# A product of the coming units behind each transpose of attention, in a fixed order

## The chip, the cores and the metric

The kernel runs on one core of a Trainium2 chip. The metric is the time of one launch in microseconds of the device; the times shown are the median of three runs. The engines that matter here are TensorE (PE: matmuls, with the weight loads shown as PEld), VectorE (DVE), ScalarE (ACT), GpSimd (POOL) and the queue of SyncE (SP), which issues most loads.

## The reference

One hybrid decoder block on x of 512 x 1024, float32: an RMS norm, one wide input projection, two attention branches of 8 heads of 64 each, and a gated merge with an output projection and a residual add.

```python
h = rms_norm(x, norm_g)
fq, fk, fv, fz, mq, mk, mv, mz, ga, gb, fl = split_cols(h @ w_in, IN_SPLITS)
q, k = rms_norm(heads(fq), fox_q_g), rms_norm(heads(fk), fox_k_g)
log_f = log_sigmoid(fl + b_f)                     # causal decay, cumulated over positions
y_fox = softmax(q k^T * scale + c_i - c_j, causal) v * silu(fz)
q, k = rope(rms_norm(heads(mq), moba_q_g)), rope(rms_norm(heads(mk), moba_k_g))
y_moba = softmax over the own block of 256 (causal) and up to 3 chosen earlier blocks * silu(mz)
merged = sigmoid(ga + b_gate0) * (y_fox @ w_fox) + sigmoid(gb + b_gate1) * (y_moba @ w_moba)
out = x + merged @ w_out
```

With 512 positions there are two blocks of 256, so the chosen blocks are all the earlier ones and the moba branch is a plain causal softmax too.

## The kernel before

Every float32 product is made of three matmuls in the fp32r type: an operand is split into a high part (a copy by ACT: the names wh, Gh, QS, KH, pth) and a low part (a subtraction, mostly by DVE: wl, Gl, KL, ptl), and high x high, high x low and low x high are accumulated in one PSUM tile.

**Units.** The input projection is cut into units. A unit of fq, fk, fv, mq, mk or mv (`unit`) makes one block of 128 positions and 256 columns: 8 k-tiles x 3 = 24 matmuls of 256 columns into a PSUM tile with tag `pj`, of which there are two, and then its copy out (`evac_qk`, `evac_v`). A unit of fz or mz (`unit_z`) makes 24 matmuls of 512 columns, one of w_fox (`unit_f`) 12 of 512 columns. I call their matmuls products. `unit_mm` (L308), `tr_mm` (L407) and `br_mm` (L691) issue them; L315 to L317, L414 to L416 and L696 to L698 are their lines in the profile. A chunk of weights is loaded by SP and split ahead of use by `pump` (L189), which is called before each unit.

**Attention.** There are four groups of four heads (fox a, fox b, moba a, moba b), each of two pairs. `Tr(pr)` (L526) transposes q and k of a pair: four transposes into the PSUM tile p_qT (L530) and four into p_kT (L532); ACT and DVE then make QS, KH, KL of each head from these two tiles. `Aa(h)` makes the logits of a head, four PSUM tiles lg (tag `lg`, two buffers) of 128, 256, 384 and 512 columns, two matmuls each (L572, L573); DVE takes the maximum and ACT the exp, into p0 to p3. `Bb(h)` (L610) transposes the ten blocks of p that the causal mask leaves (L617, by `blk`): four into p_a, four into p_b, two into p_cc; each tile is split by `spl` into pth (ACT) and ptl (DVE), and pv is accumulated from them in a fixed order (L627, L628). p_qT, p_kT, p_a, p_b, p_cc and p_ri (the transpose of the inverse sums) share the tag `tp` of three PSUM buffers; pv has one buffer.

**What sets the order.** Each engine runs its own queue in order. A scheduler lays the instructions of the program on the engines, by readiness in its own estimate and by their place in the program; `tc.issue_after(i)` ties an instruction behind instruction i on its engine, and `behind()` (L119) ties behind the last one that the program issued on an engine. In the program the pieces of attention (`Tr`, `Aa`, `Bb`, `Yp`) alternate with units (`inter`, L1034): while group n is computed, the units that group n + 1 needs are the filler (`plan`, L1074). The scheduler is free to put the units' products between the transposes, logits and pv matmuls as these become ready.

Of the kernel before, what the change touches and what calls it, by code (L numbers as in the profile page):

```python
# [13 lines left out]
P = 128  # L14
# [15 lines left out]
def fox_moba_kernel(ctx: ExitStack, tc, xT, x, w_in, w_fl, w_fox, w_moba, w_out, cst, rope, out):  # L30
# [60 lines left out]
    def col(c, n=1):  # L91
        return cs[:, c:c + n]
# [212 lines left out]
        for i, (a, b) in enumerate(pairs):  # L305
            T.matmul(o, a, b, start=(i == 0), stop=(i == n - 1))

    def unit_mm(p, name, t, hfs=(0, 1), first=True, last=True):  # L308
        n = 264 if name == "fka" else CW
        for hf in hfs:  # L310
            hi, lo = chunks[name][hf]
            for k in range(4):
                kk = 4 * hf + k
                st = slice(t * P, (t + 1) * P)
                T.matmul(p[:, :n], Gh[:, kk, st], hi[:, k, :n], start=(kk == 0), stop=False)  # L315
                T.matmul(p[:, :n], Gh[:, kk, st], lo[:, k, :n], start=False, stop=False)
                T.matmul(p[:, :n], Gl[:, kk, st], hi[:, k, :n], start=False, stop=(kk == KT - 1))  # L317

    def evac_qk(p, name, t):
        if name not in QN:  # L320
# [75 lines left out]
    def unit(name, t):  # L396
        def go():
            p = pj(f"pj_{name}{t}")
            unit_mm(p, name, t)
            if name[1] == "v":  # L400
                evac_v(p, name, t)
            else:
                evac_qk(p, name, t)
        return go


    def tr_mm(p, name, c):  # L407
        cc = slice(c * P, (c + 1) * P)
        for hf in range(2):
            hi, lo = chunks[name][hf]  # L410
            for k in range(4):
                kk = 4 * hf + k
                gh, gl = Z[kk] if name[0] == "f" else (Gh[:, kk, :], Gl[:, kk, :])
                T.matmul(p, hi[:, k, cc], gh, start=(kk == 0), stop=False)  # L414
                T.matmul(p, hi[:, k, cc], gl, start=False, stop=False)
                T.matmul(p, lo[:, k, cc], gh, start=False, stop=(kk == KT - 1))  # L416

    ZS = {}

# [2 lines left out]
    def unit_z(name, c):  # L422
        def go():
            p = (tp if name == "fzb" else pj)(f"pz_{name}{c}")
            tr_mm(p, name, c)
            z = t2("y", 15, f"zs_{name}{c}")
            s = t2("y", 15, "sg") if name == "mzb" else t2("u", 4, "sg")
            if name[0] == "f":
                V.tensor_tensor(out=z, in0=p, in1=rbc, op=OP.mult)
                A.activation(s, z, AF.Tanh, scale=0.5)  # L430
                V.scalar_tensor_tensor(z, s, 1.0, z, op0=OP.add, op1=OP.mult)
            else:
                A.activation(s, p, AF.Tanh, scale=0.5)
                V.scalar_tensor_tensor(z, s, 1.0, p, op0=OP.add, op1=OP.mult)
            ZS[name[0], 2 * (name[2] == "b") + c] = z
        return go


    LR = con.tile([64, S], F32R, name="LR")
# [77 lines left out]
    def attn_group(br, half, gq, gk):  # L517
# [8 lines left out]
        def Tr(pr):  # L526
            def go():
                pq, pk = tp("p_qT"), tp("p_kT")
                for t in range(NT):
                    T.transpose(pq[:, t * P:(t + 1) * P], qn[:, t, pr * P:(pr + 1) * P], ident)  # L530
                for t in range(NT):
                    T.transpose(pk[:, t * P:(t + 1) * P], kn[:, t, pr * P:(pr + 1) * P], ident)  # L532
                for o in range(2):
                    h = 2 * pr + o
                    me, ot = (slice(0, HD), slice(HD, P)) if o == 0 else (slice(HD, P), slice(0, HD))
                    qs = t2("qs", 4, "QS", dt=F32R)
                    kh = t2("qs", 4, "KH", dt=F32R)
                    kl = KLt[o][pr]
                    A.activation(qs[me, :], pq[me, :], AF.Copy, scale=gq[me, :])
                    V.scalar_tensor_tensor(qs[ot, :], pq[me, :], gq[me, :], qs[me, :].bitcast(F32),  # L540
                                           op0=OP.mult, op1=OP.subtract)
                    A.activation(kh[me, :], pk[me, :], AF.Copy, scale=gk[me, :])
                    if direct:
                        A.activation(kh[ot, :], pk[me, :], AF.Copy, scale=gk[me, :])  # L544
                    else:
                        nc.scalar.dma_start(out=kh[ot, :].bitcast(F32), in_=kh[me, :].bitcast(F32))
                    V.scalar_tensor_tensor(kl[me, :], pk[me, :], gk[me, :], kh[me, :].bitcast(F32),  # L547
                                           op0=OP.mult, op1=OP.subtract)
                    q2 = qs
                    if fox:  # L550
                        q2 = Q2t[o]
                        lr = slice(HD, HD + 4) if o == 0 else slice(0, 4)
                        hh = hb + h
                        nc.sync.dma_start(out=q2[lr, :].bitcast(F32), in_=LR[hh:32:8, :].bitcast(F32))
                        nc.sync.dma_start(out=kl[lr, :].bitcast(F32), in_=LR[32 + hh:64:8, :].bitcast(F32))
                        if direct:
                            V.tensor_copy(q2[me, :], qs[me, :].bitcast(F32))
                        else:
                            nc.scalar.dma_start(out=q2[me, :].bitcast(F32), in_=qs[me, :].bitcast(F32))
                    st[h] = (qs, kh, kl, q2)  # L560
            return go
# [48 lines left out]
        def Bb(h):  # L610
            def go():
# [2 lines left out]
                pv = pst("pv", 1, "pv")  # L614

                def blk(dst, i, j):
                    T.transpose(dst, pts[i][:, j * P:(j + 1) * P], ident)  # L617

                def spl(p, n):
                    tag, w, bufs = ("pt", 512, 4) if n == 512 else ("pc", 256, 2)  # L620
# [67 lines left out]

    FS, MG = {}, {}

    def br_mm(p, name, br, c):  # L691
        hi, lo = chunks[name][0]
        cc = slice(c * P, (c + 1) * P)
        for k in range(4):
            yh, yl = Y[br, k]
            T.matmul(p, hi[:, k, cc], yh, start=(k == 0), stop=False)  # L696
            T.matmul(p, hi[:, k, cc], yl, start=False, stop=False)  # L697
            T.matmul(p, lo[:, k, cc], yh, start=False, stop=(k == 3))  # L698

    def unit_f(i, c):  # L700
        def go():
            j = 2 * i + c
            p = pj(f"pf{j}")
            br_mm(p, f"wf{i}", "f", c)
            if j == 0:
                f = sb.tile([P, 4, S], F32, name="f03", tag="v", bufs=2)
                FS[0], FS[1] = f[:, 0:2, :], f[:, 2:4, :]
            elif j in (4, 6):
                FS[j // 2] = sb.tile([P, 2, S], F32, name=f"f{j}", tag="qk", bufs=4)
            A.activation(FS[i][:, c, :], p, AF.Copy)  # L710
        return go
# [121 lines left out]
    def merge_a(i, c):  # L833
        if True:
            j = 2 * i + c
            p = pj(f"pm{j}")
            br_mm(p, f"wm{i}", "m", c)
            u = SG[i][:, c, :]
            V.tensor_tensor(out=u, in0=p, in1=u, op=OP.mult)
            V.tensor_tensor(out=u, in0=u, in1=FS[i][:, c, :], op=OP.add)  # L840
# [180 lines left out]
            return [unit_z(name, c) for c in range(2)]  # L1021
        return [unit(name, t) for t in range(4)]

    def filler(names):
        res = []
        for nm in names:
            for n, u in enumerate(units(nm)):
                def go(i=first_prep[nm] + (n if nm[0] == "G" else 0), u=u):
                    pump(i)
                    u()  # L1030
                res.append(go)
        return res

    def inter(a, b):  # L1034
# [30 lines left out]
    for k, u in enumerate(fz):  # L1065
        u()
        if k < 3:
# [7 lines left out]
            ("f", "b", C_FQ, C_FK, ["mka", "mva", "mza"]),  # L1075
            ("m", "a", C_MQ, C_MK, ["mqb", "mkb", "mvb"]),
            ("m", "b", C_MQ, C_MK, ["mzb", "wf0", "wf1", "wf2"]))
    head, body, tail, gate = attn_group("f", "a", col(C_FQ), col(C_FK))
    head[0]()
    for n in range(4):  # L1080
        nxt = []

        def following(n=n, nxt=nxt):
            br, half, cq, ck = plan[n + 1][:4]
            if n == 1:
                moba_begin()
            nxt.extend(attn_group(br, half, col(cq), col(ck)))
            nxt[0][0]()
        fill = filler(plan[n][4])
        if n == 0:  # L1090
            for k in range(4):
                store = []

                at = 3 * k

                def with_sums(u=fill[at], k=k, store=store):
                    u()
                    with tc.issue_after(last_on(mybir.EngineType.DVE)):
                        store.append(make_sums(k))

                def with_store(u=fill[at + 1], store=store):
                    u()
                    store[0]()
                fill[at], fill[at + 1] = with_sums, with_store
        inter(body + ([following] if n < 3 else []) + tail, fill)
        if n < 3:
            at = 2
            body, tail = nxt[1][:at] + gate + nxt[1][at:], nxt[2]
            gate = nxt[3]
    seq(["wf3"])  # L1110
    enter("gates")
    load_sums()
    fill = filler(["GA0", "GA1", "GB0"])
# [123 lines left out]
```

## Time and profile before

| what | value |
|---|---|
| median of three runs | 425.62 us (425.09 to 425.78) |
| the profiled execution | 425.94 us, span 424.2 us |
| granted TensorE clock | 0.999 |
| PE busy | 417.8 us |
| DVE busy | 327.4 us |
| ACT busy | 279.2 us |
| matmuls | 2913 |

The span runs from the first to the last instruction; about 1.7 us of the execution lie outside it. A row of the groups reads: line, engine, operation, out<-in, shapes, count, then busy time, mean of one in ns, and the idle time just before them with what ended it. A row in order of time reads: start, length, engine, line, operation, tiles, shapes, count. The length of a matmul includes its passage through the array, in which the next one already runs; the distance between two starts is what one costs. Attention lies between 66 and 285 us.

### The profile page before, as it was taken

The numbers are of one execution on the slowest core, as the hardware profiler recorded it, in microseconds if no ns is written. First come the engines' busy times: TensorE is split into PE (matmuls) and PEld (weight loads), VectorE is DVE, ScalarE is ACT, GpSimd is POOL, SyncE is SP. The second block draws the span as 40 slices with busy tenths as digits, with TensorE's granted clock in tenths as the row PEclk, the third lists the DMA queues.
The fourth block names the chain that finished last, engine by engine and source line by source line (L and its number), as shares of the span: only waits on it lengthen the run. The fifth ranks groups of instructions, "written<-read, shape, count | busy, mean of one in ns | idle before, by whom it ended". The sixth has DMA issues, their size and how long they took to land.

```text
span 424.2 us, 7682 instructions
## 1 busy us (share of the span) xinstructions
PE 417.8 (98%) x2913; PEld 388.6 (92%) x2913; DVE 327.4 (77%) x574; ACT 279.2 (66%) x527; POOL 103.8 (24%) x120
## 2 busy tenths in 40 slices
PE   8999999999999999999999999999999999999996
PEld 6998899999999998899998888899999989988885
DVE  3779977799967778678666679767979698689883
ACT  4976326778777878569757687656756535686450
POOL 1065630225235550015660100340000000022230
PEclk9999999999999999999999999999999999999999
DMA  7972334667253033212032310673052703697484
GB/s 233 392 281 87 112 100 111 181 206 199 74 176 114 26 102 100 80 45 99 27 100 68 106 53 27 229 250 117 24 178 62 236 2 110 208 259 118 99 140 159
DMA packets 24340, 56.10 MB, mean 132 GB/s; under 512 B 2808, under 2 KB 7600, under 8 KB 24304
## 3 DMA queue, kind: packets, MB, share of 16 engines
q1 hardware_dynamic: 13392, 38.11, 27.9%
q0 software_dynamic: 3392, 8.39, 8.7%
q10 hardware_dynamic: 7520, 9.11, 6.7%
q8 instruction: 23, 0.38, 0.4%
q14 instruction: 13, 0.11, 0.1%
HBM read 48.11 MB, written 6.32 MB: 128 GB/s over the span
## 4 chain that ended last, share of the span: by engine, by line
PE 96%; DMA 1%; SPq 0%; DVE 0%; issue 0%; ACT 0%
PE pb_GB L770 3%; PE pb_GA L770 3%; PE pb_GA L767 3%; PE pb_GB L767 3%; PE pb_GB L769 3%; PE pb_GA L769 3%; PE po L958 3%; PE po L957 3%; PE po L956 3%; PE pv L628 2%; PE lg L573 2%; PE pv L627 2%; PE lg L572 2%; PE pf L697 2%; PE pf L696 2%; PE pm L698 2%
## 5 line engine op out<-in xcount | busy, mean ns | idle before, releaser
L343 POOL TENSOR_TENSOR ff<-ss,mh 128x8 f32<-128x8 f32 x16 | 31.6, 1981 | 71.4 <-DVE ss L341 62.9
L575 DVE CUSTOM_DVE_ANT_0 p<-lg,mask 128x128 f32<-128x128 f32 (+1 forms) x64 | 30.9, 487 | 16.1 <-PE lg L573 15.6
L577 ACT ACTIVATE p<-p,negm 128x128 f32<-128x128 f32 (+1 forms) x64 | 35.7, 559 | 10.9 <-DVE negm L575 10.0
L905 POOL DMA_DIRECT2D wr_o<-in_w_out_dram x4 | 4.9, 1294 | 95.5 <-ACT wr_o L904 95.5
L143 DVE TENSOR_TENSOR wl_GA<-wr_ga,wh_GA 128x1024 fp32r<-128x1024 f32 x14 | 16.9, 1223 | 5.8 <-ACT wh_GA L141 3.9
L141 ACT ACTIVATE wh_GA<-wr_ga 128x1024 fp32r<-128x1024 f32 x14 | 14.7, 1061 | 9.9 <-PE pb_GA L769 5.1
L141 ACT ACTIVATE wh_GB<-wr_gb 128x1024 fp32r<-128x1024 f32 x14 | 14.6, 1059 | 9.5 <-PE pm L697 3.5
L918 ACT ACTIVATE wh_o<-wr_o 128x1024 fp32r<-128x1024 f32 x14 | 14.8, 1060 | 7.9 <-PE pb_GB L769 2.8
L572 PE MATMUL lg<-KH,QS 128*128 128x128 f32 (+1 forms) x64 | 20.0, 324 | 0.0
L919 DVE TENSOR_TENSOR wl_o<-wr_o,wh_o 128x1024 fp32r<-128x1024 f32 x14 | 17.0, 1222 | 3.8 <-ACT wh_o L918 3.8
L143 DVE TENSOR_TENSOR wl_GB<-wr_gb,wh_GB 128x1024 fp32r<-128x1024 f32 x14 | 16.9, 1222 | 3.5 <-ACT wh_GB L141 3.5
L653 DVE TENSOR_TENSOR ypair<-pv,ysh 64x512 f32<-64x512 f32 x16 | 11.0, 687 | 6.7 <-ACT ysh L652 6.3
L547 DVE SCALAR_TENSOR_TENSOR KL<-p_kT,cs,KH 64x512 fp32r<-64x512 f32 x16 | 12.0, 749 | 3.4 <-ACT KH L544 3.2
L652 ACT ACTIVATE ysh<-pv 64x512 f32<-64x512 f32 x16 | 9.5, 594 | 7.3 <-PE pv L628 4.2
L624 DVE TENSOR_TENSOR ptl<-p_a,pth 128x512 fp32r<-128x512 f32 x16 | 11.0, 685 | 4.2 <-ACT pth L623 4.2
L337 DVE TENSOR_REDUCE ss<-sq 128x8 f32<-128x512 f32 x16 | 10.9, 681 | 4.0 <-ACT sq L336 3.9
L767 PE MATMUL pb_GA<-Gh,wh_GA 128*128 128x256 f32 x48 | 13.6, 284 | 0.0
L769 PE MATMUL pb_GA<-Gl,wh_GA 128*128 128x256 f32 x48 | 13.5, 281 | 0.0
L770 PE MATMUL pb_GA<-Gh,wl_GA 128*128 128x256 f32 x48 | 13.5, 281 | 0.0
L770 PE MATMUL pb_GB<-Gh,wl_GB 128*128 128x256 f32 x48 | 13.5, 281 | 0.0
L769 PE MATMUL pb_GB<-Gl,wh_GB 128*128 128x256 f32 x48 | 13.4, 281 | 0.0
L767 PE MATMUL pb_GB<-Gh,wh_GB 128*128 128x256 f32 x48 | 13.3, 281 | 0.0
(461 smaller groups left out, 1801.8 us busy)
## 6 DMA issues: line engine op xcount, KB each, us to landing
wr_ga<-in_w_in_dram SPq DMA_DIRECT2D x8, 512.0 KB, 3.8
wr_gb<-in_w_in_dram SPq DMA_DIRECT2D x8, 512.0 KB, 4.6
wr_o<-in_w_out_dram SPq DMA_DIRECT2D x8, 512.0 KB, 11.4
xt<-in_xT_dram SPq DMA_DIRECT2D x8, 256.0 KB, 7.3
x<-in_x_dram SPq DMA_DIRECT2D x8, 256.0 KB, 6.0
s_dramh<-sum_sh ACTq DMA_DIRECT2D x8, 256.0 KB, 5.6
s_draml<-sum_sl ACTq DMA_DIRECT2D x8, 256.0 KB, 2.5
wr_wf<-in_w_fox_dram SPq DMA_DIRECT2D x4, 512.0 KB, 3.2
```

What stands on the lines that cost most here:

```text
L141: A.activation(hi[:, :, 0:n], src, AF.Copy)
L143: eng.tensor_tensor(out=lo[:, q, 0:n], in0=src[:, q], in1=hi[:, q, 0:n].bitcast(F32), op=OP.subtract)
L343: G.tensor_tensor(out=f2, in0=ss.rearrange("p t h -> p (t h)"), in1=mh, op=OP.pow)
L572: T.matmul(lg[:, :n], qs[:, qt], kh[:, :n], start=True, stop=False)
L575: V.tensor_tensor_reduce(pt, lg[:, :n], mask[:, 512 - n:512], -0.125, 3.0e38, op0=OP.add, op1=OP.min, accum_out=mkn[:, hh, i:i + 1])
L577: A.activation(pt, pt, AF.Exp, bias=mkn[:, hh, i:i + 1], scale=-1.0, accum_out=rs[:, hh, i:i + 1])
L767: T.matmul(o, hi[:, k, cc], lh, start=(n < 3 and c == 0 and k == 0), stop=False, skip_group_check=True)
L769: T.matmul(o, hi[:, k, cc], ll, start=False, stop=False, skip_group_check=True)
L770: T.matmul(o, lo[:, k, cc], lh, start=False, stop=(k == 3), skip_group_check=True)
L918: A.activation(wide(hi), wide(R[key, c]), AF.Copy)
L919: V.tensor_tensor(out=wide(lo), in0=wide(R[key, c]), in1=wide(hi).bitcast(F32), op=OP.subtract)
L956: T.matmul(o, gh, hi[:, c, r, :], start=(new and k == 0), stop=False, skip_group_check=True)
```

## The change

The functions that issue a unit's products become generators that yield operand pairs, and `products` issues one matmul at each step. A unit becomes an object `Unit` that can be advanced by one product (`step`) or run to its end (`run`). The units that are the filler of attention, and w_fox's last, stand in a list AHEAD in the order of their use. The transposes of q and k and of p go through `turn`: it issues the transpose, tied behind the last instruction issued on PE unless it is the first of its row, and then steps the first unit of AHEAD that is not done, its product tied behind the transpose. What is left of a unit is issued where the unit stood before. The number of transposes and of products is the same, and so are their operands.

```diff
-    def unit_mm(p, name, t, hfs=(0, 1), first=True, last=True):
+    def unit_mm(name, t):
         n = 264 if name == "fka" else CW
-        for hf in hfs:
-            hi, lo = chunks[name][hf]
-            for k in range(4):
-                kk = 4 * hf + k
-                st = slice(t * P, (t + 1) * P)
-                T.matmul(p[:, :n], Gh[:, kk, st], hi[:, k, :n], start=(kk == 0), stop=False)
-                T.matmul(p[:, :n], Gh[:, kk, st], lo[:, k, :n], start=False, stop=False)
-                T.matmul(p[:, :n], Gl[:, kk, st], hi[:, k, :n], start=False, stop=(kk == KT - 1))
+        st = slice(t * P, (t + 1) * P)
+        for kk in range(KT):
+            hi, lo = (w[:, kk % 4, :n] for w in chunks[name][kk // 4])
+            gh, gl = Gh[:, kk, st], Gl[:, kk, st]
+            yield from ((gh, hi), (gh, lo), (gl, hi))
+
+    def products(o, pairs):
+
+        pairs = list(pairs)
+        for i, (a, b) in enumerate(pairs):
+            if i:
+                yield
+            T.matmul(o, a, b, start=(i == 0), stop=(i == len(pairs) - 1))
...
             p = pj(f"pj_{name}{t}")
-            unit_mm(p, name, t)
+            yield from products(p[:, :264 if name == "fka" else CW], unit_mm(name, t))
...
+    AHEAD = []
+
+    def turn(o, i, first):
+        if first:
+            T.transpose(o, i, ident)
+        else:
+            with behind(mybir.EngineType.PE):
+                T.transpose(o, i, ident)
+        while AHEAD and AHEAD[0].done:
+            AHEAD.pop(0)
+        if AHEAD:
+            with behind(mybir.EngineType.PE):
+                AHEAD[0].step()
+
+    class Unit:
+        def __init__(self, i, go):
+            self.i, self.go, self.it, self.done = i, go, None, False
+
+        def step(self):
+            if self.it is None:
+                self.it = self.go()
+            if self.it is None or next(self.it, self) is self:
+                self.done = True
+
+        def run(self):
+            pump(self.i)
+            while not self.done:
+                self.step()
...
                 for t in range(NT):
-                    T.transpose(pq[:, t * P:(t + 1) * P], qn[:, t, pr * P:(pr + 1) * P], ident)
+                    turn(pq[:, t * P:(t + 1) * P], qn[:, t, pr * P:(pr + 1) * P], t == 0)
                 for t in range(NT):
-                    T.transpose(pk[:, t * P:(t + 1) * P], kn[:, t, pr * P:(pr + 1) * P], ident)
+                    turn(pk[:, t * P:(t + 1) * P], kn[:, t, pr * P:(pr + 1) * P], False)
...
                 def blk(dst, i, j):
-                    T.transpose(dst, pts[i][:, j * P:(j + 1) * P], ident)
+                    turn(dst, pts[i][:, j * P:(j + 1) * P], j == 0 and i == 0)
...
-    def filler(names):
+    def filler(names, ahead=False):
         res = []
         for nm in names:
             for n, u in enumerate(units(nm)):
-                def go(i=first_prep[nm] + (n if nm[0] == "G" else 0), u=u):
-                    pump(i)
-                    u()
-                res.append(go)
+                x = Unit(first_prep[nm] + (n if nm[0] == "G" else 0), u)
+                if ahead:
+                    AHEAD.append(x)
+                res.append(x.run)
         return res
...
+    fills = [filler(p[4], True) for p in plan]
+    wf3 = filler(["wf3"], True)
...
-        fill = filler(plan[n][4])
+        fill = fills[n]
...
-    seq(["wf3"])
+    for u in wf3:
+        u()
```

More of the change, by code (lines that the diff above doesn't have):

```diff
@@ L404, in unit, with tr_mm @@
         return go
-    def tr_mm(p, name, c):
+    def tr_mm(name, c):
         cc = slice(c * P, (c + 1) * P)
[L409 to L416, printed above, removed]
+        for kk in range(KT):
+            hi, lo = (w[:, kk % 4, cc] for w in chunks[name][kk // 4])
+            gh, gl = Z[kk] if name[0] == "f" else (Gh[:, kk, :], Gl[:, kk, :])
+            yield from ((hi, gh), (hi, gl), (lo, gh))
     ZS = {}
@@ L424, in go @@
             p = (tp if name == "fzb" else pj)(f"pz_{name}{c}")
-            tr_mm(p, name, c)
+            yield from products(p, tr_mm(name, c))
             z = t2("y", 15, f"zs_{name}{c}")
@@ L689, in fox_moba_kernel, with br_mm @@
     FS, MG = {}, {}
-    def br_mm(p, name, br, c):
+    def br_mm(name, br, c):
         hi, lo = chunks[name][0]
@@ L695, in br_mm @@
             yh, yl = Y[br, k]
-            T.matmul(p, hi[:, k, cc], yh, start=(k == 0), stop=False)
-            T.matmul(p, hi[:, k, cc], yl, start=False, stop=False)
-            T.matmul(p, lo[:, k, cc], yh, start=False, stop=(k == 3))
+            yield from ((hi[:, k, cc], yh), (hi[:, k, cc], yl), (lo[:, k, cc], yh))
     def unit_f(i, c):
@@ L703, in go @@
             p = pj(f"pf{j}")
-            br_mm(p, f"wf{i}", "f", c)
+            yield from products(p, br_mm(f"wf{i}", "f", c))
             if j == 0:
@@ L836, in merge_a @@
             p = pj(f"pm{j}")
-            br_mm(p, f"wm{i}", "m", c)
+            for _ in products(p, br_mm(f"wm{i}", "m", c)):
+                pass
             u = SG[i][:, c, :]
```

## The prediction, on record before the run

> **What bounds the kernel now.** I read the page first, then the list of waits of PE (TensorE's matrix multiply queue), then busy time by stretch, then single instructions in order of time.
>
> ```profile
> span 424.2 us, 7682 instructions
> ...
> PE 417.8 (98%) x2913; PEld 388.6 (92%) x2913; DVE 327.4 (77%) x574; ACT 279.2 (66%) x527; POOL 103.8 (24%) x120
> ...
> PEclk9999999999999999999999999999999999999999
> ...
> PE 96%; DMA 1%; SPq 0%; DVE 0%; issue 0%; ACT 0%
> ```
> ```profile
> PE warm_ps L107 <- DVE fg_pre L480: 1.5, 1, 1.5
> PE fqa L392 <- DVE wl_fqa L168: 0.7, 1, 0.7
> PE fqa L391 <- ACT Zh L131: 0.6, 1, 0.6
> ```
> ```profile
> 66.00:112.00 46.00, 46.00 (x378) 45.31 (x377) 40.98 (x92) 35.12 (x80) 13.00 (x9) 1.00 0.59 169
> 112.00:162.00 50.00, 50.00 (x409) 49.22 (x408) 37.81 (x81) 39.52 (x83) 21.68 (x29) 1.00 0.30 96
> 162.00:216.00 54.00, 54.00 (x394) 50.68 (x393) 40.00 (x83) 40.89 (x88) 17.83 (x21) 1.00 0.27 88
> 216.00:285.00 69.00, 69.00 (x425) 61.16 (x423) 49.44 (x97) 49.00 (x102) 14.48 (x18) 1.00 0.33 108
> ```
>
> The chain that ends last is PE for 96% of the span. The three waits shown are all that PE has, and all lie in the first 12 us. Attention runs from 66 to 285 us, and there PE is busy for the whole of every stretch (46.00 of 46.00, and so on; the columns after the length are PE, weight loads, DVE, ACT, POOL, then clock and DMA). So in attention the time is the sum of what PE is given, and it can change in two ways only: an instruction takes PE less or more time, or PE has to wait. The second has nothing to gain there. VectorE (DVE) and ScalarE (ACT) are not idle: 40.98 and 35.12 of the first 46 us, 37.81 and 39.52 of the next 50.
>
> **Part 1: a product behind each transpose, as a price on PE.** Matmuls overlap, so I price one by the distance between starts.
>
> ```profile
> 66.03 0.60 PE L530 MATMUL p_qT<-ident,qn_fqa 128*128 128x128 f32 x4
> 66.47 0.60 PE L532 MATMUL p_kT<-ident,qn_fka 128*128 128x128 f32 x4
> ...
> 67.03 0.28 PE L316 MATMUL pj_fqb<-wl_fqb,Gh 128*128 128x256 f32 x1
> ...
> 72.47 0.29 PE L317 MATMUL pj_fqb<-wh_fqb,Gl 128*128 128x256 f32 x1
> ...
> 74.92 0.22 PE L572 MATMUL lg<-KH,QS 128*128 128x128 f32 x1
> 74.98 0.28 PE L573 MATMUL lg<-KL,Q 128*128 128x128 f32 x1
> 75.09 0.33 PE L572 MATMUL lg<-KH,QS 128*128 128x256 f32 x1
> ...
> 84.22 0.34 PE L573 MATMUL lg<-KL,Q 128*128 128x384 f32 x1
> 84.39 0.27 PE L617 MATMUL p_a<-ident,p 128*128 128x128 f32 x1
> ...
> 84.62 0.28 PE L316 MATMUL pj_fkb<-wl_fkb,Gh 128*128 128x256 f32 x1
> ```
>
> From 67.03 to 72.47 stand 46 products: 5.44 / 46 = 0.118 us each. From 66.03 to 67.03 stand eight transposes in a row and one product: (1.00 - 0.118) / 8 = 0.110 us a transpose. From 84.39 to 84.62 stand one transpose, alone among other work, and one product: 0.23 - 0.118 = 0.11 us. A transpose alone costs what one in a row does. The change makes rows into single ones, 224 of them (4 groups, each 16 of q and k and 40 of p), 221 of which then have a product next; the count of matmuls and products stays. Price of part 1: 224 x 0 = 0. The bounds: if the next weight load were hidden wholly, a transpose would cost its stream alone, 0.06 us (74.92 to 74.98, also 128 columns): -224 x 0.05 = -11.2 us; if the switch between kinds cost a hundredth of a microsecond, +2.2. I take 0, since the single row at 84.39 is the very case.
>
> [...]
>
> **Part 2: the tied order.** Before, products not yet needed are free work, which the scheduler puts wherever PE would otherwise wait. Now ten of them go with each head's p transposes and eight with each pair's q and k; each such product is held behind its transpose and each transpose but a row's first behind the product ahead of it, and as products of one tile accumulate in order, the rest of that unit is held as well. The program of the changed kernel can be listed by engine, and there free work has gone from several places between a transpose and what needs its copy. A PE instruction that waits for a copy holds the whole queue behind it. I follow four such places, with these prices.
>
> ```profile
> 140.13 0.39 PE L573 MATMUL lg<-KL,Q 128*128 128x512 f32 x1
> 140.36 0.60 PE L532 MATMUL p_kT<-ident,qn_fkb 128*128 128x128 f32 x4
> ...
> 140.99 0.69 ACT L542 ACTIVATE KH<-p_kT,cs 64x512 fp32r<-64x512 f32 x1 [0.22 <-PE p_kT L532]
> ```
> ```profile
> L577 ACT ACTIVATION_READ_ACCUMULATOR p<-p,negm 128x1 f32 x64 | 12.1, 190 | 0.0
> L577 ACT ACTIVATE p<-p,negm 128x512 f32<-128x512 f32 x16 | 11.5, 720 | 1.8 <-DVE negm L575 1.7
> ...
> L542 ACT ACTIVATE KH<-p_kT,cs 64x512 fp32r<-64x512 f32 x16 | 10.9, 680 | 1.2 <-PE p_kT L532 1.0
> ...
> L623 ACT ACTIVATE pth<-p_a 128x512 fp32r<-128x512 f32 x16 | 9.5, 595 | 0.6 <-PE p_a L617 0.3
> ...
> L141 ACT ACTIVATE wh_mza<-wr_mza 128x1024 fp32r<-128x1024 f32 x2 | 2.1, 1060 | 0.0
> ...
> L680 ACT ACTIVATE yhm<-ypair 128x512 fp32r<-128x512 f32 x3 | 1.9, 629 | 2.0 <-DVE ypair L679 2.0
> L599 ACT ACTIVATE rinv_t<-p_ri 8x128 f32<-8x128 f32 x7 | 1.8, 260 | 3.2 <-PE p_ri L597 2.5 <-PE lg L573 0.7
> ...
> L322 ACT ACTIVATE qn_fkb<-pj_fkb 128x256 f32<-128x256 f32 x4 | 1.5, 379 | 0.0
> ```
> ```profile
> L540 DVE SCALAR_TENSOR_TENSOR QS<-p_qT,cs,QS 64x512 fp32r<-64x512 f32 x16 | 12.0, 750 | 1.5 <-ACT QS L539 1.0
> ...
> L624 DVE TENSOR_TENSOR ptl<-p_a,pth 128x512 fp32r<-128x512 f32 x16 | 11.0, 685 | 4.2 <-ACT pth L623 4.2
> ...
> L575 DVE CUSTOM_DVE_ANT_0 p<-lg,mask 128x256 f32<-128x256 f32 x16 | 6.7, 420 | 4.0 <-PE lg L573 4.0
> ...
> L575 DVE CUSTOM_DVE_ANT_0 p<-lg,mask 128x128 f32<-128x128 f32 x16 | 4.6, 288 | 3.5 <-PE lg L573 3.3
> ...
> L143 DVE TENSOR_TENSOR wl_mza<-wr_mza,wh_mza 128x1024 fp32r<-128x1024 f32 x2 | 2.5, 1226 | 0.8 <-ACT wh_mza L141 0.7
> ...
> L557 DVE CAST Q<-QS 64x512 fp32r<-64x512 f32 x4 | 2.1, 536 | 0.1
> ```
>
> The last of four transposes starts at 140.36 + 3 x 0.11 = 140.69 and ACT takes up its tile at 140.99: a lag of 0.30. QS on ACT and KL on DVE have KH's and QS's shapes, so I give them 0.68 and 0.75. A matmul of 512 columns stands 0.23 apart (140.13 to 140.36), one of 384 0.17, one of 128 0.11.
>
> *Place C, the fox b group's second pair.* Time 0 is the start of the last p_kT transpose. PE then has 17 products, four pairs of p_a transpose and product, four lg matmuls: p_b's first transpose is due at 0.11 + 2.01 + 0.91 + 0.45 = 3.48. Its tile comes free when DVE has read p_qT for the second head. ACT, in its order: 0.30, KH 0.98, KH 1.66, wh_mza 2.72, QS 3.40, qn_mka 3.78, wh_mza 4.84, KH 5.52, KH 6.20, pth 6.80. DVE: wl_mza 2.72 to 3.95, QS 4.70, Q 5.23, the p of lg 128 with 0.08 for its sums 5.60, wl_mza 6.83, the p of lg 256 7.33, KL 8.08. So p_b waits 4.70 - 3.48 = 1.22; four pairs and lg 384 twice bring PE to 5.95, and pv waits for pth until 6.80: 0.85; lg 512 then stands at 7.03 and waits for the second p, 7.33: 0.30; after its 0.46, p_cc stands at 7.79 and waits for KL, 8.08: 0.29. Sum 2.7 us. Before, 23 products stand between p_a and p_b here, 23 x 0.118 = 2.7 us of cover.
>
> *Place B, the moba b group's first pair.* From the last p_qT transpose to pv listed 1.6 us (two pairs of p_kT, four of p_a, the products); ACT in that order does QS 0.68, yhm 0.63, an exp 0.72 + 0.19, pth 0.60 after the lag of 0.30: 3.1. Wait 1.5. Then p_b needs p_a's tile, which ptl frees 0.69 after pth; 0.68 later its last transpose starts, lag and pth 0.90: 2.27, where the list has 0.23 + 0.91 + 0.23 = 1.37. Wait 0.9.
>
> *Place E, the moba b group's second pair.* From the last p_kT transpose to p_b listed 0.34 + 4 x 0.34 + 0.45 = 2.15; p_qT comes free after lag, KH, KH, QS on ACT and QS on DVE: 0.30 + 3 x 0.68 + 0.75 = 3.09. Wait 0.9.
>
> *Place A, fox a.* Of fkb the second unit's end has moved behind the third's. ACT copies it out after rinv_t: from p_ri's start 0.30 + 0.26 + 0.38 = 0.94, and the product that takes that tile is listed 0.11 after p_ri. Wait 0.8.
>
> Sum of the four: 2.7 + 2.4 + 0.9 + 0.8 = 6.8 us. The same walk finds smaller ones (the q and k chains of fox b and moba a, the rest of place E, and at B the POOL chain that ends in the last two p_kT transposes); I have no one row for their queues and put them at a quarter, 1.7: in all 8.5. Bounds: with nothing queued ahead on ACT, B's pv still waits 0.30 + 0.60 - 0.23 = 0.67, A 0.8, E 0.9 and C's first wait 0.6 (half): 3.0. Upward: if each of eight pairs paid what C does, 21.6; half of that beyond the four, say 18.
>
> **Part 3: what else moves.**
>
> ```profile
> L143 DVE TENSOR_TENSOR wl_fqb<-wr_fqb,wh_fqb x2: 1212/1214/1217, 53.8 to 56.5; 128x1024 fp32r<-128x1024 f32 x2
> ```
>
> Weight chunks are used up to 1.1 us earlier (ten products of 0.118); loads and splits keep their order, and a q and k load of SP stands one place earlier among weight loads: 0. The first products brought forward, fqb's, have their chunks split by 56.5 + 1.2 = 57.7 us, 8 us ahead of the first transpose at 66.03. Zero, or a loss within the 1.7.
>
> **Sum.** The profiled execution took 425.94 us for a span of 424.2 (1.7 around it) and the median is 425.62, 0.3 less. 425.94 + 0 + 8.5 + 0 = 434.4, by the median's level 434.1.
>
> **Rivals.** *Hidden weight loads, on the other side:* in the alternating order a transpose streams under the products' loads and costs 0.06. From parts 1 and 2: -11.2 + 8.5 = -2.7, 422.9 us; it decides from 0.038 us saved a transpose (8.5 / 224). For it, weight loads start as soon as the matmul before has started; against it, the row at 84.39. Chance 0.07. [...] *No waits:* the engines get through sooner than my walk, as they start the copies of p_qT with the row half done; part 1 at zero gives 425.6. Against it, ACT and DVE have little to spare. Chance 0.06. *Waits everywhere:* a late PE makes ACT and DVE late for the next pair too, since DVE is already busy 41 of 46 us, and each pair pays as C: 425.6 + 18 = 443.6. Chance 0.19. The change is in the listed order (221 transposes with a product next, 34 before), so that it does nothing is no rival.
>
> **How the numbers follow.** My forecast, some waits and no cheaper transposes, has 0.68, with a range of its own from 428.6 (3.0) to 439. The stated range runs from 428.6 to 443.6 and leaves out the first two rivals and the far side of the third. What this measurement tells from no change is about 0.2%, 0.9 us. Faster 0.07, within 0.05, slower 0.88.
>
> **What would show it.** Right: PE's list of waits gains ACT and DVE releasers for pv, p_b, p_cc, lg and pj in 66 to 285 us, 6 to 10 us in all, the largest near the second pair of fox b and in moba b; PE's busy time falls below the stretch's length; a transpose and product stand 0.23 apart. Wrong: pairs 0.18 apart (the loads are hidden), or PE without a wait in attention. Wrong in size: waits in every pair.

## The result and the profile after

| | before | after |
|---|---|---|
| median | 425.47 us (425.09 to 425.78, 4 runs) | 435.47 us (434.91 to 437.62, 4 runs) |
| profiled execution, span | 425.94 us, 424.2 us | 437.62 us, 435.6 us |
| start of the first and the last matmul | 1.55, 420.30 us | 1.55, 431.71 us |

The changed kernel is slower: the ratio is 1.0248, with a 95% interval of 1.0233 to 1.0262. The predicted time was 434.1 us, in a range of 428.6 to 443.6. The page of the profile after, its busy times and the chain that ended last:

```profile
span 435.6 us, 7688 instructions
...
PE 424.7 (97%) x2913; PEld 390.6 (90%) x2913; DVE 330.0 (76%) x574; ACT 278.3 (64%) x527; POOL 104.3 (24%) x120
...
PE 86%; DVE 5%; ACT 4%; DMA 2%; issue 1%; ACTq 0%; SPq 0%; DVEq 0%
```

The number of matmuls is the same. PE's share of the chain fell from 96% to 86%, and DVE and ACT came in: at some places PE now waits for them. The list of waits of PE in the changed kernel (total, times, longest):

```profile
PE p_b L448 <- DVE QS L572: 1.8, 2, 1.5
PE warm_ps L107 <- DVE fg_pre L512: 1.5, 1, 1.5
PE pv L659 <- ACT pth L655: 1.4, 3, 0.6
PE fqa L396 <- ACT Zh L131: 0.6, 1, 0.6
PE pj_fvb L322 <- DVE v_fvb L358: 0.6, 1, 0.6
PE pj_mvb L322 <- DVE v_mvb L358: 0.3, 1, 0.3
PE pj_mkb L322 <- ACT qn_mqb L327: 0.3, 1, 0.3
PE lg L605 <- DVE KL L579: 0.3, 1, 0.3
PE p_b L448 <- DVE ptl L656: 0.2, 1, 0.2
```

All but the rows of warm_ps and fqa lie in attention, where the list of before was empty. And the four stretches of attention, where PE was busy for the whole length before:

```profile
66.00:112.00 46.00, 45.38 (x369) 44.42 (x369) 38.42 (x83) 32.48 (x75) 14.07 (x9) 1.00 0.56 169
112.00:162.00 50.00, 48.05 (x374) 46.18 (x373) 41.26 (x87) 39.04 (x84) 22.17 (x29) 0.97 0.29 96
162.00:216.00 54.00, 53.72 (x389) 50.02 (x388) 36.59 (x74) 38.73 (x81) 12.54 (x17) 1.00 0.21 69
216.00:285.00 69.00, 66.67 (x398) 56.58 (x396) 49.53 (x99) 48.23 (x102) 15.60 (x20) 1.00 0.27 92
```

PE is idle for 0.6, 1.9, 0.3 and 2.3 us, 5.2 us in all. That is half of what was lost: both views count a wait only from the modelled end of the matmul before it, and they leave out work that was slower. The distance between starts shows the whole of a wait. Place B in order of time:

```profile
223.49 0.27 PE L445 MATMUL p_a<-ident,p 128*128 128x128 f32 x1
224.10 0.39 PE L322 MATMUL pj_mvb<-wh_mvb,Gh 128*128 128x256 f32 x1 [0.34 <-DVE v_mvb L358]
...
224.81 0.36 PE L322 MATMUL pj_mvb<-wh_mvb,Gh 128*128 128x256 f32 x1
225.74 0.49 PE L659 MATMUL pv<-pth,v_mva 128*128 128x512 f32 x1 [0.57 <-ACT pth L655]
226.46 0.33 PE L448 MATMUL p_b<-ident,p 128*128 128x128 f32 x1 [0.23 <-DVE ptl L656]
...
227.45 0.39 PE L660 MATMUL pv<-ptl,v_mva 128*128 128x512 f32 x1
228.18 0.44 PE L659 MATMUL pv<-pth,v_mva 128*128 128x384 f32 x1 [0.34 <-ACT pth L655]
```

A transpose costs 0.11, and the product behind it starts 0.61 later: 0.50 lost, of which 0.34 is listed. In the same way, pv loses 0.73 (0.93 between starts, 0.20 for the product ahead of it, which is recorded right behind its transpose), p_b 0.49 (0.72 less 0.23) and the last pv 0.50 (0.73 less 0.23). Together 2.2 us.

Counted so over the whole trace, with the distances that the same kinds have before, the 11.4 us between the two last matmuls (431.71 - 420.30) are made up of:

| where | us |
|---|---|
| place C: p_b 1.63, pv 0.63, lg 512 0.21 | 2.5 |
| place B | 2.2 |
| place E: lg for KL 0.50, p_b for QS 0.60, twice 0.26 after it | 1.6 |
| waits for a tile of a unit: 105 us 0.78, 201 us 0.44; and p_b at 121 us 0.18 | 1.4 |
| a lower granted clock behind place C, without the wait of lg 512 that falls into it | 1.5 |
| some 0.003 more for a transpose with its product, 221 times | 0.7 |
| the first 12 us: products of fqa stand 0.12 apart from 6.8 us on before, from 10.7 us on after, and the listed waits of fqa are 1.3 us before, 0.6 after | 0.6 |
| small rest, most of it about 0.1 right behind the waits | 0.9 |

### The profile page after: what moved, and what is told of

Same layout as the page of the kernel before. It is cut to its first block, busy times and chain, and to the rows that moved or that the text cites. A ratio compares the mean times of both kernels' runs of the same rounds, so it can differ in the third digit from the quotient of the medians.

```text
span 435.6 us, 7688 instructions
## 1 busy us (share of the span) xinstructions
PE 424.7 (97%) x2913; PEld 390.6 (90%) x2913; DVE 330.0 (76%) x574; ACT 278.3 (64%) x527; POOL 104.3 (24%) x120
## 4 chain that ended last, share of the span: by engine, by line
PE 86%; DVE 5%; ACT 4%; DMA 2%; issue 1%; ACTq 0%; SPq 0%; DVEq 0%
PE pm L322 5%; PE pf L322 5%; PE pb_GB L800 3%; PE pb_GA L800 3%; PE pb_GB L797 3%; PE pb_GA L797 3%; PE pb_GB L799 3%; PE pb_GA L799 3%; PE po L989 3%; PE po L988 3%; PE po L987 3%; PE pj_mkb L322 3%; PE pj_fva L322 3%; PE pj_mqa L322 3%; PE pj_mqb L322 3%; PE pj_mva L322 3%
## 5 line engine op out<-in xcount | busy, mean ns | idle before, releaser
L348 POOL TENSOR_TENSOR ff<-ss,mh 128x8 f32<-128x8 f32 x16 | 29.9, 1875 | 67.4 <-DVE ss L346 57.4
L609 ACT ACTIVATE p<-p,negm 128x128 f32<-128x128 f32 (+1 forms) x64 | 35.7, 558 | 11.0 <-DVE negm L607 10.7
L448 PE MATMUL p_b<-ident,p 128*128 128x128 f32 x64 | 16.2, 274 | 2.1 <-DVE QS L572 1.8
L572 DVE SCALAR_TENSOR_TENSOR QS<-p_qT,cs,QS 64x512 fp32r<-64x512 f32 x16 | 12.0, 750 | 5.0 <-ACT QS L571 4.6
L571 ACT ACTIVATE QS<-p_qT,cs 64x512 fp32r<-64x512 f32 x16 | 10.9, 682 | 5.1 <-PE p_qT L448 1.9
L656 DVE TENSOR_TENSOR ptl<-p_b,pth 128x512 fp32r<-128x512 f32 x16 | 11.0, 685 | 4.0 <-ACT pth L655 3.9
L322 PE MATMUL pf<-yhf,wh_wf 128*128 128x512 f32 x32 | 13.9, 440 | 0.0
L322 PE MATMUL pf<-yhf,wl_wf 128*128 128x512 f32 x32 | 13.9, 434 | 0.0
```

The lines of the kernel that those rows point to most:

```text
L322: T.matmul(o, a, b, start=(i == 0), stop=(i == len(pairs) - 1))
L348: G.tensor_tensor(out=f2, in0=ss.rearrange("p t h -> p (t h)"), in1=mh, op=OP.pow)
L609: A.activation(pt, pt, AF.Exp, bias=mkn[:, hh, i:i + 1], scale=-1.0, accum_out=rs[:, hh, i:i + 1])
L656: V.tensor_tensor(out=lo[:, :n], in0=p[:, :n], in1=hi[:, :n].bitcast(F32), op=OP.subtract)
```

## The experiments

All are variants of the changed kernel, with the kernel before timed beside them on the same chip. Its medians there were 425.32 us for the first four, 425.27 for the next four, 425.66 for the next three and 425.74 for the last. "Pairs" are transposes that have a product next in PE's queue: 34 before, 221 after.

**1 and 2. No ties, and no products behind.** The same source, with both ties left out; and the transposes tied, but nothing stepped behind them.

```diff
 notie
-        if first:
-            T.transpose(o, i, ident)
-        else:
-            with behind(mybir.EngineType.PE):
-                T.transpose(o, i, ident)
+        T.transpose(o, i, ident)
...
-            with behind(mybir.EngineType.PE):
-                AHEAD[0].step()
+            AHEAD[0].step()
 noprod
-        if AHEAD:
-            with behind(mybir.EngineType.PE):
-                AHEAD[0].step()
```

> The products are still issued between the transposes in the program, but without either tie; the scheduler places them. 86 transposes have a product next (34 before, 221 in the changed kernel). Theory (the ties take away the free products that cover copies): 425 to 427.5 us, PE without a wait over 0.3 us in attention. Rival (a transpose next to a product costs more by itself): the loss of 10 us goes with the number of such pairs, (86 - 34) / (221 - 34) = 28% of it, 428.3 us.

> Ties alone: each transpose is tied behind the one before it in its row, and no product is moved. The order of PE has 34 transposes with a product next, as before. Theory: 425.5 us, the time of before, since a tie that holds no product takes no cover away. Rival (a tied row by itself makes waits): 428 us or more.

Measured: without ties 426.05 us (425.82 to 426.64), ratio 1.002 (1.001 to 1.0029). Without products 425.32 us, ratio 1.0001 (0.9991 to 1.0012). The first has no wait of PE after the first 12 us. So neither the generators nor a tie of transposes among themselves costs anything worth a name, and a product issued behind a transpose without a tie costs 0.7 us, less than a tenth of the loss (86 pairs; by the pair it would be 2.8).

**3 and 4. One kind of transpose alone.** `turn` for q and k only, then for p only; the other kind as before.

```diff
 qk
-                    turn(dst, pts[i][:, j * P:(j + 1) * P], j == 0 and i == 0)
+                    T.transpose(dst, pts[i][:, j * P:(j + 1) * P], ident)
 p
-                    turn(pq[:, t * P:(t + 1) * P], qn[:, t, pr * P:(pr + 1) * P], t == 0)
+                    T.transpose(pq[:, t * P:(t + 1) * P], qn[:, t, pr * P:(pr + 1) * P], ident)
...
-                    turn(pk[:, t * P:(t + 1) * P], kn[:, t, pr * P:(pr + 1) * P], False)
+                    T.transpose(pk[:, t * P:(t + 1) * P], kn[:, t, pr * P:(pr + 1) * P], ident)
```

> Only the 64 transposes of q and k take a product behind them, in the tied order; those of p stand in rows as before. Theory: the p tiles' waits at moba b go, a part of those of p_b on QS stays: 427 to 430 us. Rival (price by pairs, 78 of them): 425.5 + 24% of 10 = 427.9 us. This run tells where the loss is rather than which theory holds.

> Only the 160 transposes of p take a product behind them, in the tied order; those of q and k stand in rows. Theory: the waits of pv on pth and of p_b on its tile stay in most places: 430 to 434 us. Rival (price by pairs, 166 of them): 425.5 + 71% of 10 = 432.6 us. With the run on q and k alone it shows whether the two parts add up to the whole 10 us; by waits they need not, by pairs they do.

Measured: q and k alone 428.07 us, ratio 1.0057 (1.0036 to 1.0079); p alone 430.04 us, ratio 1.0106 (1.0086 to 1.0127, from three executions; a fourth took 1060.7 us, and the record does not show why). The losses of 2.7 and 4.7 us add to 7.4, not to the 10 us of both. The first fits a price by the pair too (427.9 us), the second does not (432.6). A price by the pair would add up; waits need not, since one kind's free products can cover the other kind's copies.

**5 and 6. One of the two ties alone.**

```diff
 trtie
-            with behind(mybir.EngineType.PE):
-                AHEAD[0].step()
+            AHEAD[0].step()
 prodtie
-        if first:
-            T.transpose(o, i, ident)
-        else:
-            with behind(mybir.EngineType.PE):
-                T.transpose(o, i, ident)
+        T.transpose(o, i, ident)
```

> Only the transposes are tied, each behind what PE was given before it; the product behind it is free to go elsewhere (112 with a product next). At place C 21 products are back between p_a's last transpose and lg, and 13 more before p_b. Theory (what is lost is the free product): 425.5 to 429 us, no wait at C. Rival by the pair: 425.3 + 10.1 x (112 - 34) / (221 - 34) = 429.5 us.

> Only the products are tied, each behind its transpose; the transposes are free (175 with a product next). At place C one product stands between p_a's last transpose and the lg ahead of p_b, as in the changed kernel. Theory: the waits at C stay, 430 to 435 us. Rival by the pair: 425.3 + 10.1 x (175 - 34) / (221 - 34) = 432.9 us; rival that the transposes' tie is what costs: near 426 us.

Measured: transposes tied 426.09 us, ratio 1.0027 (1.0013 to 1.0042), though 112 pairs are left; products tied 432.33 us, ratio 1.0171 (1.0156 to 1.0186). It is the product's tie that costs: 7 of the 10 us; the transposes' tie alone costs 0.8, and some 2 us come only with both. The products' tie taken alone would fit a price by the pair (432.9 us), the transposes' tie would not (429.5). With the products tied PE still waits at place C, but for other copies than in the changed kernel: for the maximum ahead of lg 384, for pth, and for KL ahead of p_cc.

```profile
147.15 0.44 PE L600 MATMUL lg<-KH,QS 128*128 128x384 f32 x1 [0.89 <-DVE negm L603]
...
148.59 0.50 PE L655 MATMUL pv<-pth,v_fvb 128*128 128x512 f32 x1 [0.35 <-ACT pth L651]
149.52 0.30 PE L444 MATMUL p_cc<-ident,p 128*128 128x128 f32 x1 [0.43 <-DVE KL L575]
```

The windows of 138 to 160 us, place C, in the kernel with tied transposes and in the changed kernel:

```profile
138.00:160.00 22.00, 22.00 (x180) 21.45 (x179) 17.37 (x41) 17.11 (x38) 16.26 (x21) 1.00 0.19 62
```
```profile
138.00:160.00 22.00, 20.07 (x149) 18.93 (x149) 16.77 (x37) 17.00 (x36) 14.45 (x20) 0.92 0.19 66
```

With free products PE is busy for all 22.00 us; with tied ones it lacks 1.9 us, gets 31 matmuls fewer done, and the granted clock is 0.92.

**7 and 8. Another unit's products behind the transposes.** The alternation and both ties are kept, but the tied product comes from the second unit that is still undone, so that the first one's stay free: in all groups, then in fox b alone.

```diff
 next
+        nx = [x for x in AHEAD if not x.done]
-        if AHEAD:
+        if nx:
             with behind(mybir.EngineType.PE):
-                AHEAD[0].step()
+                nx[min(1, len(nx) - 1)].step()
 nextfb
+                nx[min(SKIP[0], len(nx) - 1)].step()
...
     for n in range(4):
+        SKIP[0] = int(n == 1)
```

> Alternation and both ties are kept (220 of 224 transposes have a product next), but the product tied behind a transpose comes from the second unit still undone, so that the first one's 24 products stay free; at place C 51 products and two transposes now stand between the last p_kT transpose and p_a's third. Theory (the lost cover is the loss): the waits at C go, most of the 10 us come back, 427 to 431 us. Rival (the alternation itself, or the tie, costs by the pair): 435 us as the changed kernel.

> As the changed kernel in fox a, moba a and moba b; in the fox b group alone the tied product comes from the second unit still undone, as in the run that did so everywhere. Alternation and ties stay in all groups (219 of 224 transposes with a product next); at place C 42 products lie between p_a's first two transposes. Theory (the place of free products decides, not the pair): C's waits and the lower clock behind it go as when fox b was plain, 431 to 433 us, PE without a wait in 138 to 160 us and a clock of 1.00 there; the waits at 105 us and in moba b stay. Rival by the pair: 435.3 us. Rival that a later place pays it back: 434 to 435.5 us with more waits after 160 us.

Measured: in all groups 434.67 us, ratio 1.0222 (1.0206 to 1.0237): the theory's 427 to 431 missed. In fox b alone 432.88 us, ratio 1.0172 (1.0155 to 1.0189), inside 431 to 433. At place C both did what was expected. Place C, window and PE in order of time, with the tied product from the second unit in fox b alone:

```profile
138.00:160.00 22.00, 22.00 (x182) 21.64 (x181) 17.00 (x40) 17.21 (x39) 13.96 (x21) 1.00 0.20 62
```
```profile
142.06 0.27 PE L445 MATMUL p_a<-ident,p 128*128 128x128 f32 x1
...
147.49 0.27 PE L448 MATMUL p_a<-ident,p 128*128 128x128 f32 x1
```

The 41 products (42 were expected) and four lg matmuls between p_a's first two transposes (142.06 to 147.49) do again what the free products did before: no wait, every transpose of the place still with a product next or ahead of it. So what costs at C is the place of the free products, not the pair. Why the same rule lost elsewhere is seen in the waits of the kernel that used it everywhere, and of the one that used it in fox b:

```profile
PE lg L605 <- DMA KH<-KH: 1.6, 1, 1.6
...
PE pj_mvb L322 <- DVE v_mvb L358: 1.3, 2, 0.9
PE pf L322 <- ACT f L741: 0.9, 1, 0.9
```
```profile
PE pj_mkb L322 <- ACT qn_mqb L327: 0.8, 1, 0.8
...
PE pj_mqb L322 <- DVE zs_mza L435: 0.3, 1, 0.3
```

Two units are now open at a time, which takes both pj buffers, and a product that needs the next one waits for a copy out (v_mvb, f, qn_mqb, zs_mza). At the very start of attention the products of the first two units were used up before lg, which then stood with no cover for KH's transfer. The cover had been moved, not made.

**9 to 11. One group left out, and one group alone.** Plain transposes in fox b; in all groups but fox b (`!= "fb"`); in moba b (`== "mb"`).

```diff
+        plain = br + half == "fb"
...
-    def turn(o, i, first):
+    def turn(o, i, first, plain=False):
+        if plain:
+            T.transpose(o, i, ident)
+            return
...
-                    turn(dst, pts[i][:, j * P:(j + 1) * P], j == 0 and i == 0)
+                    turn(dst, pts[i][:, j * P:(j + 1) * P], j == 0 and i == 0, plain)
```

The two calls of `turn` for q and k get `plain` in the same way.

> Plain transposes in the fox b group alone, alternation and ties in the other three (175 with a product next). Theory: place C's 2.7 us go, and with them the stretch of lower clock where there was one; the waits of moba b stay: 430 to 433 us; PE without a wait in 138 to 160 us. Rival by the pair: 435.5 - 10.1 x 46 / 187 = 433.0 us. Rival that a later place pays what C no longer does: 434 to 435.5 us.

> Alternation and ties in the fox b group alone, plain transposes in the other three (78 with a product next). Theory: the waits of place C alone, 2.7 us, and at most the 4.0 us that came back when the fox b group was made plain: 428 to 429.5 us, PE without a wait after 162 us. If a wait of 1.5 us at C lowers the granted clock, the windows behind it show less than 1.00 and the span some 2 us more. Rival by the pair: 425.3 + 10.1 x (78 - 34) / (221 - 34) = 427.7 us.

> Plain transposes in the moba b group alone, alternation and ties in the other three (174 with a product next). Theory: places B and E go, where the changed kernel's PE lost about 4.9 us between 216 and 285 us: 435.5 - 4.9 = 430.6 us, 429.5 to 431.5; PE without a wait in 216 to 285 us. Rival by the pair: 435.5 - 10.1 x 47 / 187 = 433.0 us.

Measured: fox b plain 431.44 us, ratio 1.0147 (1.013 to 1.0164), as expected; PE has no wait in 138 to 160 us, and somewhat more after it (by starts about 0.9 us in 160 to 216, against 0.6). Fox b alone 430.25 us, ratio 1.0113 (1.0085 to 1.0141): 0.75 above the range for the waits alone, because all four of its executions had a clock of 0.992 to 0.996; less some 1.5 us for the clock (below) it is about 3 us of waits, where the prediction had 2.7. They are not the predicted waits: the largest is lg 384's for the maximum of an earlier lg, in front of p_b, and p_b itself then waits only 0.26 for QS.

```profile
146.04 0.44 PE L608 MATMUL lg<-KH,QS 128*128 128x384 f32 x1 [1.62 <-DVE negm L611]
```

Moba b plain 432.37 us, ratio 1.0165 (1.0138 to 1.0192): 3.1 us came back, not 4.9. Place E is gone, but B stays; B in that kernel:

```profile
226.65 0.50 PE L663 MATMUL pv<-pth,v_mva 128*128 128x512 f32 x1 [0.56 <-ACT pth L659]
227.37 0.33 PE L451 MATMUL p_b<-ident,p 128*128 128x128 f32 x1 [0.23 <-DVE ptl L660]
```

The tile v_mva says why: the p transposes of this place belong to moba a's last head, which runs while moba b's first q and k are transposed. Taking the group out of the alternation did not take the place out; the expectation had read "moba b's first pair" as if all of its work were moba b's.

With these, 78 pairs cost 2.7 us (q and k alone) or 4.6 (fox b alone), 112 cost 0.8, 174 cost 6.7 (moba b plain), 175 cost 7.1 (products tied) or 6.2 (fox b plain), and 219 to 221 cost 7.1 (fox b with the second unit's products), 9.4 (everywhere) or 10. There is no price by the pair. None of the variants is faster than the kernel before; it has no wait in attention to give up.

**12. The changed kernel again.**

> The changed kernel once more, for its clock: 434.9 to 435.9 us where the granted clock stays at 1.00, about 2 us more where the windows behind place C show less than 1.00 as in the first profile; the waits at C, B and E in the same places, that of C's p_b 1.5 us.

Measured: 435.48 us, ratio 1.023 (1.0208 to 1.0252), the same waits at the same places, p_b's at C listed with 1.45. Its profiled execution took 436.32 us with a clock of 0.996, about 1 us more than the others, not 2; the other three, at 0.998 to 1.000, took 434.94 to 435.84.

## Why the prediction was right, and where it was not

**What bounds the kernel** held: attention was the sum of PE's work, and the change could only add to it. No variant came below.

**Part 1, a product behind each transpose at 0,** held. The first transposes of attention in the changed kernel:

```profile
66.52 0.27 PE L445 MATMUL p_qT<-ident,qn_fqa 128*128 128x128 f32 x1
66.55 0.37 PE L322 MATMUL pj_fqb<-wh_fqb,Gh 128*128 128x256 f32 x1
66.75 0.27 PE L448 MATMUL p_qT<-ident,qn_fqa 128*128 128x128 f32 x1
...
66.98 0.27 PE L448 MATMUL p_qT<-ident,qn_fqa 128*128 128x128 f32 x1
```

A transpose and its product stand 0.23 apart (66.52, 66.75, 66.98), as at 84.39 before; over the pairs with a product of 256 columns it is 0.231 in the mean, against 0.228 for the two by themselves (0.118 and 0.110), some 0.7 us in all. That the product is recorded 0.03 behind its transpose is no overlap: the next transpose makes it up. The rival of hidden weight loads, with 0.18 for a pair, falls.

**Part 2, the cover that the ties take away,** is the cause, and the runs show it rather than the trace alone: the product's tie costs 7 of the 10 us, the transposes' alone 0.8, and the free products given back at C end C's waits with every tie in place. By its places:

*Place C* went as it was walked through. DVE and ACT around it in the changed kernel, and PE:

```profile
146.14 1.39 DVE L143 TENSOR_TENSOR wl_mza<-wr_mza,wh_mza 128x1024 fp32r<-128x1024 f32 x1 [0.35 <-ACT wh_mza L141]
147.56 0.76 DVE L572 SCALAR_TENSOR_TENSOR QS<-p_qT,cs,QS 64x512 fp32r<-64x512 f32 x1
```
```profile
149.75 0.60 ACT L655 ACTIVATE pth<-p_a 128x512 fp32r<-128x512 f32 x1
```
```profile
143.32 0.27 PE L448 MATMUL p_kT<-ident,qn_fkb 128*128 128x128 f32 x1
...
148.46 0.30 PE L448 MATMUL p_b<-ident,p 128*128 128x128 f32 x1 [1.47 <-DVE QS L572]
...
150.40 0.64 PE L659 MATMUL pv<-pth,v_fvb 128*128 128x512 f32 x1 [0.47 <-ACT pth L655]
```

From the last p_kT transpose at 143.32, the walk had QS done at 4.70; it was done at 148.32, 5.00 later, since wl_mza took 1.39 instead of 1.23 and started 0.10 late. It had pth done at 6.80, measured 7.03. The waits of PE: p_b 1.63 (1.22 predicted), pv 0.63 (0.85), lg 512 0.21 (0.30), and p_cc, put at 0.29, was hidden in the lower clock. The sum is 2.5 against 2.7. In two of the variants the same place cost PE other waits (above), so the amount is better founded than the order of the waits.

*Place B* 2.2 against 2.4, but of three waits that only the total caught: the 1.5 ahead of pv came as 0.50 ahead of a product and 0.73 ahead of pv, and the 0.9 of p_b as 0.49 there and 0.50 at the next pv.

*Place E* was under-counted: p_b for QS 0.60 of the 0.9, but 1.0 us more around it that the prediction had left in its quarter.

*Place A* failed, and with it a term of 0.8. The step that failed is that "the product that takes that tile" waits for ACT's copy. The rows of the changed kernel:

```profile
93.16 0.27 PE L629 MATMUL p_ri<-ident,rinv 128*8 128x128 f32 x1
...
93.19 0.37 PE L322 MATMUL pj_fkb<-wh_fkb,Gh 128*128 128x256 f32 x1
```
```profile
94.08 0.36 ACT L327 ACTIVATE qn_fkb<-pj_fkb 128x256 f32<-128x256 f32 x1
```

The product runs 0.9 us before that copy begins, so it did not need that tile. Why the prediction took it to need it (perhaps by letting the two pj buffers change hands in strict turns) no row shows. The mechanism was right and the place wrong; waits of this kind came at 105 us (0.78) and 201 us (0.44), and at B.

*The smaller ones*, put at 1.7, came to 1.4 with those two and p_b at 121 us, beside E's rest. So the waits add to 7.7 us in place of 8.5. That the total came so near is in part luck: A's 0.8 fell away, E cost 0.7 more than its own term, and B's three waits differ one by one.

**Part 3, the earlier use of the chunks, at 0,** held: no wait of PE in attention is for a chunk of weights. (Ten products of 0.118 are 1.2 us, not 1.1.)

**What the sum had no term for**: the lower clock (1.5 us in the profiled execution), and 2.2 us of pairs, start and small rest. The timed executions at full clock, 434.91 to 435.87, lie above 434.1 by these small terms.

**The rivals.** "No waits" falls by the list of waits. "Waits everywhere" falls too: by starts PE lost about 1.3 us from 66 to 142 us and 0.6 from 160 to 216, and the rest of the loss sits in three places. One sign was named too high: the list of waits holds 4.9 us in attention, not 6 to 10, because it counts from the modelled end of a matmul; by the distances between starts it is 7.7.

## What to carry over

Where one engine is busy all the time, work that nothing waits for is worth its place: count for each instruction that needs another engine's copy how much free work stands between, and compare that with the copy's queue, before an order is tied. Tie, if at all, the instructions that must be early, and leave the free ones free; here the first cost 0.8 us and the second 7. Read what a wait costs from the distance between starts, and check by the tile names whose work a stretch holds before an experiment takes a group out.

## What was not expected of the hardware

Behind the wait at place C the granted clock of TensorE fell to 0.50 for 3.4 us. Windows of one microsecond of the changed kernel (PE, weight loads, DVE, ACT, POOL, then the granted clock):

```profile
147.00:148.00 1.00, 0.00 (x0) 0.00 (x0) 0.97 (x2) 0.98 (x2) 0.98 (x2) 1.00 0.00 0
148.00:149.00 1.00, 0.54 (x6) 0.57 (x6) 0.94 (x3) 0.97 (x2) 0.45 (x1) 1.00 0.24 94
...
150.00:151.00 1.00, 0.60 (x2) 0.52 (x3) 0.97 (x4) 0.97 (x3) 0.00 (x0) 0.80 0.45 176
151.00:152.00 1.00, 1.00 (x5) 0.65 (x4) 0.97 (x2) 1.00 (x4) 0.00 (x0) 0.50 0.50 180
152.00:153.00 1.00, 1.00 (x7) 1.00 (x7) 1.00 (x3) 0.74 (x3) 0.52 (x1) 0.50 0.93 246
153.00:154.00 1.00, 1.00 (x6) 1.00 (x6) 1.00 (x4) 0.00 (x0) 0.00 (x0) 0.50 0.25 98
```

PE does nothing from 147 to 148 us and half of the next; two microseconds later the clock is 0.50 for 0.4 + 3 = 3.4 us, and products stand 0.21 apart (152.54, 152.75, 152.97) instead of 0.12. At half speed that is at most 1.7 us lost; by the distances between starts it was 1.5, since PE waits for a part of it anyway. The profiles of fox b alone, of moba b plain and of the changed kernel again show the same 3.4 us of 0.50 behind the same place. It does not follow every such wait: five of the eight timed executions of the changed kernel have a clock of 1.000, and a wait of 1.6 us at 73 us, in the profile with the second unit's products everywhere, was followed by 1.00.

What sets the clock no run shows. The idle time of PE in six microseconds around such places, and the clock behind them:

| kernel, stretch | idle time of PE | clock behind it |
|---|---|---|
| changed kernel, first profile, 145 to 151 us | 1.93 us | 0.50 |
| changed kernel again, 145 to 151 us | 1.91 us | 0.50 |
| fox b alone, 143 to 149 us | 1.93 us | 0.50 |
| moba b plain, 145 to 151 us | 1.92 us | 0.50 |
| products tied, 144 to 150 us | 1.67 us | 1.00 |
| second unit's products everywhere, 72 to 78 us | 1.73 us | 1.00 |

The four places with the most idle time are those with 0.50 behind them; six places make no rule. Where PE has no more work, the time to the fall differs too: from the end of the last matmul it was 1.9 us in the first profile of the changed kernel (431.99 to 433.90) and 2.6 us in that of the kernel before (420.58 to 423.20). This is read from the traces; no run moved a wait on purpose, and the executions without a trace show only a mean clock.
